# Four starting addresses for the four quarters of the transposed tokens

## The chip, the cores and the metric

The kernel runs on one core of one Trainium2 chip. The metric is the device time of one execution in microseconds. Three runs of the kernel before took 2196.5, 2198.72 and 2198.88 us; their median, 2198.72 us, is the time before. The profile shown below is of a separate execution of the same kernel, with a time of its own.

## The reference, cut to what matters

A decoder trunk of two layers on 256 tokens of width 2048, all in float32: a recurrent mixer with an MLP, then an attention mixer with an MLP, each with a norm ahead of it and a residual add behind it, and a final norm.

```python
for i in range(DEPTH):                     # DEPTH = 2
    h = _rmsnorm(x, mix_norm[i])
    x = x + (_rglru_block(h, ...) if i % 2 == 0 else _dilated_attention_block(h, ...))
    x = x + _mlp(_rmsnorm(x, mlp_norm[i]), mlp_w1[i], mlp_w2[i])
return _rmsnorm(x, final_norm)

def _mlp(h, w1, w2):                       # w1: 2048 x 8192, w2: 8192 x 2048
    u = jnp.square(jax.nn.relu(jnp.einsum('bsd,df->bsf', h, w1)))
    return jnp.einsum('bsf,fd->bsd', u, w2)
```

The recurrent block projects 2048 to 5120 (`w_in`), has block-diagonal gates, a scan over the tokens, and an output matrix of 2560 x 2048 (`w_out`). The attention block has `w_qkv` (2048 x 6144) and `w_o` (2048 x 2048). Every weight is used once, for all 256 tokens.

## The kernel before

Every weight matrix is cut on the host into units of 128 x 2048 floats (1 MB; the gates' units are half as large) and streamed through three buffers `raw`. ScalarE copies a unit to `whi` in the format that TensorE multiplies (L86), and VectorE subtracts, `wlo = raw - whi` (L90). Activations are split in the same way into a high and a low half. A product is then three matmuls: high by high, high by low, low by high. All of them go through one helper, `mm` (L142), so the profile has them on one line and tells them apart by the tiles that they read.

Two tiles carry activations into these products.

- `xT`, the tokens transposed: 2048 input rows as 16 blocks k of 128, in four tiles (quarters) `xT0` to `xT3` with four k each. A quarter has 4 x 512 floats per partition: for each k, 256 columns of high halves (one per token) and 256 of low halves. `new_xT` (L161) allocates a quarter; `transpose_chunk` (L169) fills it from the residual stream, once ahead of each of the three later sub-layers that need it, and the start of the program fills it from the host's transposed tokens.
- `aT0` to `aT19`, one tile of 512 floats for each 128 rows of a hidden activation: 256 high, 256 low.

There are two ways to multiply. In the *standing* way (`stand_w` L216, `stand_w2` L252) 128 x 128 of the weights is loaded into TensorE, and `xT` streams as the moving operand, in 256 or 512 columns; this serves `w_in` (40 units) and `w1` (64 units for each MLP, in four chunks of 16). In the *moving* way (`stand_x` L265) 128 columns of activations are loaded, and 512 columns of the weights stream; this serves `w_out`, `w2` and `w_o` with `aT`, and `w_qkv` (48 units) with `xT`. A moving unit covers four k, thus one quarter of `xT`; a standing unit covers all 16.

`stand_w2` has a style for each chunk, which sets the order of its matmuls (`orders`, L225). "h" is the high weights, "l" the low ones. For each k, "thirds" does h with the high columns, h with the low columns, l with the high columns, three matmuls of 256 columns that all add to the same 256 columns of `acc`; "thirds_low_first" starts with the l. The other styles do h with all 512 columns at once and l with 256, so that their sums come out in two halves: "wide_first" h, l; "as_was" l, h; "pairs" two k together (l, l, h, h); "fours" four h and then four l; "apart" all 16 h and then all 16 l. Columns and products are the same in each. `u_done` (L488) ends a tile: after one of the "thirds" kinds it reads 256 columns (L491), after the others it first adds the two halves (L493).

`stand_w` has the order of "thirds". The gates of the recurrent block (`gate_run`, L384) use it too, with a tile `chl` in the place of `xT`.

The order of everything is written out by hand: a list of items, one or two per unit. Before an item `before_unit` (L103) issues the loads and splits of units to come, and work on finished sums runs at fixed distances behind (`after`). Transposes (L176) and the two small transposes of `rstd_rows` (L209) run on TensorE between the items of the next chunk. Loads go through SP's queue alone.

Tiles of the pool `perm` lie one behind another in the order of first use, each rounded up to 32 bytes; the pool of the weights follows, and then the tiles of the current sub-layer. From this order and the sizes, the first bytes in a partition are:

| tile | start, bytes | modulo 512 |
|---|---|---|
| `xT0`, `xT1`, `xT2`, `xT3` | 45312, 53504, 61696, 69888 | 256 each |
| `aT0` to `aT15` | 80192 and every 2048 from there | 320 |
| `whi` (4 buffers), `wlo` (3 buffers) | 138560 and every 8192 from there | 320 |
| `chl` | 206176 | 352 |
| `aT16` to `aT19` | 220512 and every 2048 from there | 352 |

A block of 128 weights in a row is 512 bytes, a half of an activation block 1024 bytes. So for a given pair of tiles the distance modulo 512 between the moving operand and the loaded one is the same for every k and every buffer: -64 for `xT` against the weights, +32 for `chl` against the weights, and, with the weights moving, 0 against `aT0` to `aT15`, -32 against `aT16` to `aT19`, +64 against `xT`.

Of the kernel before, what the change touches and what calls it, by code (L numbers as in the profile page):

```python
# [11 lines left out]
F32R = mybir.dt.float32r  # L12
# [31 lines left out]
SOFT = (5, 3, 3, 3, 3)  # L44
LOOK_LO = 2
LOOK_HI = 3


@with_exitstack
def trunk(ctx: ExitStack, tc: tile.TileContext, a: dict, out: bass.AP):  # L50
    nc = tc.nc
    P = 128

    perm = ctx.enter_context(tc.tile_pool(name="perm", bufs=1))
# [7 lines left out]
    def unit(ap, width=UW):  # L62
        units.append((ap, width))
        return len(units) - 1
# [27 lines left out]
    def cut_hi(i):  # L92
        new_hi(i)
        for n in range(len(raw[i])):
            hi_piece(i, n)
# [7 lines left out]
    def before_unit(i):  # L103
        while seen["load"] < min(len(units), i + 1 + LOOK_LOAD):
            load(seen["load"])
            seen["load"] += 1
        while seen["hi"] < min(len(units), i + 1 + LOOK_HI):
            cut_hi(seen["hi"])
# [7 lines left out]
    def item(u, fn):  # L116
        items.append((u, fn))
# [20 lines left out]
    def after(n, fn, *args):  # L138
        later.setdefault(now[0] + n, []).append((fn, args))
# [13 lines left out]
    xc = [perm.tile([P, NT, 512], F32, name=f"xc{n}") for n in range(NCH)]  # L153
    ssq = perm.tile([P, NT, NCH], F32, name="ssq", bufs=2)
    state = {}

    def hilo(hi_out, lo_out, src):
        nc.scalar.activation(hi_out, src, AF.Copy)
        nc.vector.tensor_sub(lo_out, src, hi_out.bitcast(F32))

    def new_xT(n):  # L161
        t = perm.tile([P, 4, 512], F32R, name=f"xT{n}")
        state["xT", n] = t
        return t

# [3 lines left out]
    def transpose_chunk(n, gname):  # L169
        xg = perm.tile([P, 4, S], F32, name="xg", bufs=2)  # L170
        for b in range(2):
            tr = psum.tile([P, 2, S], F32, name="tr", bufs=2)
            for k in range(2):
                c = (2 * b + k) * 128
                for t in range(NT):
                    nc.tensor.transpose(tr[:, k, t * 128:(t + 1) * 128], xc[n][:, t, c:c + 128], ident)  # L176
            for k in range(2):
                nc.scalar.activation(xg[:, 2 * b + k, :], tr[:, k, :], AF.Identity,
                                     scale=pcol(gname, 4 * n + 2 * b + k))
        t = new_xT(n)  # L180
        for h in range(2):
            s = slice(2 * h, 2 * h + 2)
            hilo(t[:, s, 0:256], t[:, s, 256:512], xg[:, s, :])
# [68 lines left out]
    def stand_w2(ps, u, ks, w_at, first, last, style):  # L252
        hi, lo = split[u]
        todo = orders(style, ks)
        if first and todo[0][0] == "l" and not one_sum(style):

            at = next(i for i, p in enumerate(todo) if p[0] == "h")
            todo = [todo[at]] + todo[:at] + todo[at + 1:]
        for n, (w, k, c0, c1) in enumerate(todo):
            j = k - ks[0] + w_at  # L260
            s = slice(j * 128, (j + 1) * 128)
            o = ps[:, 0:256] if one_sum(style) else ps[:, c0:c1]
            mm(o, (hi if w == "h" else lo)[:, s], xT(k)[:, c0:c1], first and n == 0, last and n == len(todo) - 1)
# [12 lines left out]
    def acc_tile():  # L276
        return psum.tile([P, 512], F32, name="acc", bufs=4)
# [3 lines left out]
    def out_item(key, u, get, ks, first, last, done):  # L281
        def run():
            if first:
                accs[key] = [acc_tile() for _ in range(NT)]
            stand_x(accs[key], u, get, ks, first, last)
            if last:
                after(0, done, accs.pop(key))
        item(u, run)

    def add_x(n, acc):  # L290
        for t in range(NT):
            nc.vector.tensor_add(xc[n][:, t, :], xc[n][:, t, :], acc[t])  # L292

    def close_chunk(n, gname, rows):
        def done(acc):
            if n == 0:
                new_ssq()
            add_x(n, acc)
            if n < NCH - 1:
                square_sum(n)  # L300
            after(1, transpose_chunk, n, gname)
            if n == NCH - 1:
                after(1, square_sum, n)
                after(1, rstd_cols)
                if rows:
                    after(4, rstd_rows)
        return done
# [196 lines left out]
    def plan_mlp(w1, w2, done, styles):  # L504
        for c in range(4):
            us = []

            def part(j, ks, first, last, us=us, c=c, style=styles[c]):
                def run():
                    if first:  # L510
                        accs["u", j] = acc_tile()
                    stand_w2(accs["u", j], us[j], ks, ks[0], first, last, style)
                    if last:
                        after(1 if c == 0 and j == 0 else 0, u_done, j, accs.pop(("u", j)), style)
                item(us[j], run)

            us.extend(unit(w1[c * 16 + j]) for j in range(16))
            at = 0
            if c == 0:
                for j in range(2):  # L520
                    part(j, range(0, 12), True, False)
                for j in range(2):
                    part(j, range(12, 16), False, True)
                at = 2
            for j in range(at, 16):
                part(j, range(16), True, True)
            for n in range(NCH):
                last_c = c == 3
                if last_c and n == NCH - 1 and done is final_done:
                    final_items([unit(w2[(c * 4 + n) * 4 + kq]) for kq in range(4)])  # L530
                    continue
                for kq in range(4):
                    u = unit(w2[(c * 4 + n) * 4 + kq])
                    out_item(("m", n), u, aT, range(4 * kq, 4 * kq + 4), kq == 0, kq == 3,
                             done(n) if last_c else (lambda acc, n=n: add_x(n, acc)))
# [135 lines left out]
    def final_items(us):  # L671
        acc = {}

        def part(kq, ts):
            def run():
                if kq == 0:
                    for t in ts:
                        acc[t] = acc_tile()
                stand_x(acc, us[kq], aT, range(4 * kq, 4 * kq + 4), kq == 0, kq == 3, ts)
                if kq == 3:  # L680
                    for t in ts:
                        after(0, final_rows, acc[t], t)
            item(us[kq], run)

        part(0, range(NT))
        for t in range(NT):
            for kq in (1, 2, 3):
                part(kq, (t,))

    def load_g():  # L690
# [9 lines left out]
    item(None, lru.close)  # L700
    item(None, lambda: lru.open("mlp"))
    plan_mlp(a["w1_0"], a["w2_0"], lambda n: close_chunk(n, "mix1", False),
             ("thirds", "wide_first", "pairs", "apart"))
    item(None, lru.close)
    item(None, lambda: lru.open("att"))
    plan_att()
    item(None, lru.close)
    item(None, load_g)
    plan_mlp(a["w1_1"], a["w2_1"], final_done, ("thirds_low_first", "fours", "thirds", "as_was"))


    nc.sync.dma_start(par, a["par"])
# [16 lines left out]
    for n in range(NCH):  # L729
        xg[n] = perm.tile([P, 4, S], F32, name="xg", bufs=2)  # L730
        rs = [wts.tile([P, UW], F32, name="raw", bufs=RAW_BUFS) for _ in range(3)] if n == 0 else rs
        for h in range(2 if n == 0 else 1):
            w = 2 if n == 0 else 4
            nc.sync.dma_start(xg[n][:, h * w:(h + 1) * w, :], a["xT"][:, 4 * n + h * w:4 * n + (h + 1) * w, :])
            for i in range(3):
# [6 lines left out]
                raw[i].append((s, rs[i][:, s]))  # L742
                nc.sync.dma_start(rs[i][:, s], units[i][0][:, s])
        t = new_xT(n)
        for h in range(2 if n == 0 else 1):
            w = 2 if n == 0 else 4
# [151 lines left out]
```

## Time and profile before

| | |
|---|---|
| median of the runs | 2198.72 us (2196.5 to 2198.88, 3 runs) |
| the profiled execution | 2199.65 us, of which the span of its instructions is 2197.9 us |
| TensorE busy | 2175.3 us, 99% of the span, 12490 matmuls |
| weight loads (beside the matmuls) | 1910.4 us, 12490 |
| VectorE, ScalarE busy | 1280.0 us (58%), 1061.3 us (48%) |
| moved by DMA | 413.40 MB, 188 GB/s |
| granted TensorE clock | 0.996 |

How to read it: a busy TensorE is one with a matmul under way, not one at its peak, since a matmul's recorded duration contains a fixed latency that overlaps the next one. What a matmul costs is seen from the starts: first and last start of a group, divided by the steps between them. The view of a tile gives, for each kind of instruction, count, shortest, median and longest duration in ns, and the first and last start in us; the names of buffers and quarters are left out, so `xT0` to `xT3` are all `xT`.

| stretch of the trace, us | what runs there |
|---|---|
| 6 to 269 | recurrent block: `w_in` (standing) and gates |
| 269 to 384 | `w_out` (moving, with `aT`), the last gate |
| 384 to 1094 | first MLP: four chunks, `w1` standing and `w2` moving by turns |
| 1094 to 1387 | QKV (moving, with `xT`) and attention |
| 1387 to 1483 | `w_o` (moving, with `aT`) |
| 1483 to 2189 | second MLP, four chunks |

### The profile page before, as it was taken

How to read it: one execution, taken by the hardware profiler on the slowest of the kernel's cores; microseconds unless marked ns; L12 is line 12 of the kernel's file. 1: busy time of each engine (PE TensorE's matmuls, PEld its weight loads, DVE VectorE, ACT ScalarE, POOL GpSimd, SP SyncE). 2: the span in 40 equal slices, each digit the busy share in tenths (PEclk: the TensorE clock that was granted, in tenths of full speed). 3: DMA queues.
4: the chain of work that ended last, by engine and by line, in shares of the span. 5: the costliest groups of instructions: out<-in, count | busy, mean ns of one | idle time of the engine just before them, and what ended most of it. 6: DMA issues, size and time to landing. Idle time of an engine off the chain costs nothing.

```text
span 2197.9 us, 29494 instructions
## 1 busy us (share of the span) xinstructions
PE 2175.3 (99%) x12490; PEld 1910.4 (87%) x12490; DVE 1280.0 (58%) x1344; ACT 1061.3 (48%) x1163; POOL 78.3 (4%) x42
## 2 busy tenths in 40 slices
PE   7999999999999999999999999999999999999998
PEld 7999988998888888888888888889988889988886
DVE  8898855554564565565555555555546645545654
ACT  5787754543443343344445544555434434433442
POOL 2221100000000000000000000000000000000001
PEclk9999999999999999999999999999999999999999
DMA  6565555455555555555554445455555555555553
GB/s 219 211 211 194 194 207 189 175 192 191 191 183 201 185 188 197 189 189 194 181 192 166 159 174 183 161 188 199 200 195 181 198 196 184 186 193 189 191 192 115
DMA packets 61700, 413.40 MB, mean 188 GB/s; under 512 B 6784, under 2 KB 7168, under 8 KB 13440
## 3 DMA queue, kind: packets, MB, share of 16 engines
q1 hardware_dynamic: 61568, 411.51, 53.3%
q8 instruction: 98, 1.61, 0.3%
q14 instruction: 34, 0.28, 0.0%
HBM read 409.39 MB, written 2.10 MB: 187 GB/s over the span
## 4 chain that ended last, share of the span: by engine, by line
PE 96%; DVE 2%; ACT 1%; POOL 0%; DMA 0%; issue 0%; SPq 0%; DVEq 0%; ACTq 0%
PE acc L142 93%; PE g L142 1%; DVE wlo L90 1%; PE tr L176 0%; PE tr L568 0%; PE g L576 0%; DMA xg<-in_xT 0%; DVE xT L750 0%; PE tr L599 0%; POOL a L357 0%; ACT whi L86 0%; POOL c L358 0%; PE g L609 0%; PE g L608 0%; PE g L607 0%
## 5 line engine op out<-in xcount | busy, mean ns | idle before, releaser
L90 DVE TENSOR_TENSOR wlo<-raw,whi 128x2048 fp32r<-128x2048 f32 (+3 forms) x400 | 883.4, 2212 | 345.6 <-PE acc L142 267.9
L86 ACT ACTIVATE whi<-raw 128x2048 fp32r<-128x2048 f32 (+3 forms) x400 | 736.8, 1844 | 525.2 <-PE acc L142 437.6
L142 PE MATMUL acc<-xT,whi 128*128 128x256 f32 (+1 forms) x4064 | 882.7, 317 | 7.0 <-ACT whi L86 6.3
L142 PE MATMUL acc<-whi,aT 128*128 128x512 f32 x2624 | 813.9, 390 | 0.0
L142 PEld LDWEIGHTS acc<-xT,whi 128*128 128x128 f32 x4064 | 653.8, 190 | 46.4 <-ACT whi L86 6.7
L142 PE MATMUL acc<-xT,wlo 128*128 128x256 f32 x2672 | 654.9, 280 | 7.1 <-DVE wlo L90 6.8
L142 PEld LDWEIGHTS acc<-whi,aT 128*128 128x128 f32 x2624 | 492.6, 188 | 102.2
L142 PE MATMUL acc<-wlo,aT 128*128 128x512 f32 x1312 | 510.7, 389 | 0.0
L142 PEld LDWEIGHTS acc<-xT,wlo 128*128 128x128 f32 x2672 | 481.8, 190 | 27.6 <-DVE wlo L90 8.3
L142 PEld LDWEIGHTS acc<-wlo,aT 128*128 128x128 f32 x1312 | 246.3, 188 | 50.5
L142 PE MATMUL acc<-whi,xT 128*128 128x512 f32 x768 | 245.9, 395 | 0.0
L496 ACT ACTIVATE mu<-mr 128x256 f32<-128x256 f32 x128 | 53.5, 418 | 370.2 <-DVE mr L494 242.7
L142 PEld LDWEIGHTS acc<-whi,xT 128*128 128x128 f32 x768 | 144.3, 188 | 30.7
L142 PE MATMUL acc<-wlo,xT 128*128 128x512 f32 x384 | 150.4, 392 | 0.0
L493 DVE TENSOR_REDUCE mr<-acc 128x256 f32<-128x512 f32 x80 | 55.3, 692 | 156.1 <-PE acc L142 156.1
L292 DVE TENSOR_TENSOR xc<-xc,acc 128x512 f32<-128x512 f32 x78 | 53.2, 687 | 97.7 <-PE acc L142 97.7
L491 DVE SCALAR_TENSOR_TENSOR mr<-acc,rstdB 128x256 f32<-128x256 f32 x48 | 20.2, 424 | 112.9 <-PE acc L142 112.9
L142 PEld LDWEIGHTS acc<-wlo,xT 128*128 128x128 f32 x384 | 72.2, 188 | 15.1
L643 POOL TENSOR_TENSOR xc<-xc,gB 128x1024 f32<-128x1024 f32 x3 | 10.6, 3534 | 1879.9 <-DMA raw<-in_w 1843.4
L498 ACT ACTIVATE aT<-mu 128x256 fp32r<-128x256 f32 x128 | 53.6, 419 | 4.1
L502 DVE TENSOR_TENSOR aT<-mu,aT 128x256 fp32r<-128x256 f32 x128 | 53.4, 418 | 0.0
L189 ACT ACTIVATE junk<-xc 128x512 bf16<-128x512 f32 x32 | 20.2, 633 | 57.1 <-DVE xc L292 38.6
(143 smaller groups left out, 792.2 us busy)
## 6 DMA issues: line engine op xcount, KB each, us to landing
raw<-in_w SPq DMA_DIRECT2D x256, 1024.0 KB, 4.8
raw<-in_w_qkv SPq DMA_DIRECT2D x48, 1024.0 KB, 4.8
raw<-in_w_in SPq DMA_DIRECT2D x35, 1024.0 KB, 4.8
raw<-in_w_out SPq DMA_DIRECT2D x20, 1024.0 KB, 4.8
raw<-in_w_o SPq DMA_DIRECT2D x16, 1024.0 KB, 4.8
raw<-in_w_g SPq DMA_DIRECT2D x10, 512.0 KB, 3.3
raw<-in_w_in SPq DMA_DIRECT2D x11, 256.0 KB, 5.0
xc<-in_x SPq DMA_DIRECT2D x4, 512.0 KB, 5.7
```

Of the source, the lines that this page charges most:

```text
L86: nc.scalar.activation(split[i][0][:, s], r, AF.Copy)
L90: nc.vector.tensor_sub(split[i][1][:, s], r, split[i][0][:, s].bitcast(F32))
L142: nc.tensor.matmul(o, l, r, start=start, stop=stop, skip_group_check=True)
L189: nc.scalar.activation(junk, xc[n][:, t, :], AF.Square, accum_out=sq[:, t, n:n + 1])
L292: nc.vector.tensor_add(xc[n][:, t, :], xc[n][:, t, :], acc[t])
L491: nc.vector.scalar_tensor_tensor(r, ps[:, 0:256], 0.0, state["rstdB"], op0=OP.max, op1=OP.mult)
L493: nc.vector.tensor_reduce(r, ps.rearrange("p (b c) -> p c b", b=2), axis=AX.X, op=OP.add)
L496: nc.scalar.activation(uu, r, AF.Square)
L498: nc.scalar.activation(t[:, 0:256], uu, AF.Copy)
L502: nc.vector.tensor_sub(t[:, 256:512], uu, t[:, 0:256].bitcast(F32))
L643: nc.gpsimd.tensor_mul(xc[n], xc[n], state["gB"][:, None, n * 512:(n + 1) * 512].to_broadcast([P, NT, 512]))
```

## The change

Each quarter's tile becomes one row of 2048 floats and a pad, and the quarter's data start some floats behind its beginning. `XT_AT` holds the starts in floats (32, 128, 96 and 128 bytes), `XT_PAD` the floats added to the tile (32, 128, 96 and 256 bytes). The pads come to 512 bytes, so that all tiles behind the quarters move by 512 bytes and keep their remainder.

| quarter | starts at, bytes | modulo 512 | minus the weights' 320 |
|---|---|---|---|
| `xT0` | 45312 + 32 = 45344 | 288 | -32 |
| `xT1` | 53536 + 128 = 53664 | 416 | +96 |
| `xT2` | 61856 + 96 = 61952 | 0 | -320, the same as +192 |
| `xT3` | 70144 + 128 = 70272 | 128 | -192, the same as +320 |

With it, the styles of the chunks change: the first MLP has "as_was", "thirds", "thirds_low_first" and "apart" in place of "thirds", "wide_first", "pairs" and "apart"; the second has "thirds" in all four chunks in place of "thirds_low_first", "fours", "thirds" and "as_was". What is computed stays.

```diff
+XT_AT = (8, 32, 24, 32)
+XT_PAD = (8, 32, 24, 64)
...
     state = {}
+    xT_home = [None] * 4
...
     def new_xT(n):
-        t = perm.tile([P, 4, 512], F32R, name=f"xT{n}")
+        xT_home[n] = perm.tile([P, 2048 + XT_PAD[n]], F32R, name=f"xT{n}")
+        t = xT_home[n][:, XT_AT[n]:XT_AT[n] + 2048].rearrange("p (k c) -> p k c", k=4)
         state["xT", n] = t
         return t
...
     plan_mlp(a["w1_0"], a["w2_0"], lambda n: close_chunk(n, "mix1", False),
-             ("thirds", "wide_first", "pairs", "apart"))
+             ("as_was", "thirds", "thirds_low_first", "apart"))
...
-    plan_mlp(a["w1_1"], a["w2_1"], final_done, ("thirds_low_first", "fours", "thirds", "as_was"))
+    plan_mlp(a["w1_1"], a["w2_1"], final_done, ("thirds", "thirds", "thirds", "thirds"))
```

## The prediction

> **What bounds the kernel now.** I read the page first: how full TensorE is, and the chain that ended last.
>
> ```profile
> span 2197.9 us, 29494 instructions
> PE 2175.3 (99%) x12490; PEld 1910.4 (87%) x12490; DVE 1280.0 (58%) x1344; ACT 1061.3 (48%) x1163; POOL 78.3 (4%) x42
> ...
> PE acc L142 93%; PE g L142 1%; DVE wlo L90 1%; PE tr L176 0%; PE tr L568 0%; PE g L576 0%; DMA xg<-in_xT 0%; DVE xT L750 0%; PE tr L599 0%; POOL a L357 0%; ACT whi L86 0%; POOL c L358 0%; PE g L609 0%; PE g L608 0%; PE g L607 0%
> ```
>
> TensorE never rests, and 93% of the chain is line 142, the one helper through which every split matmul goes. So the time is the number of columns streamed times what a column costs, and the only lever this change has is that cost. I then asked for the matmuls that touch xT in two stretches that run the same instructions: a chunk of the second MLP in the style "thirds_low_first" (from its third unit on), and the one in "thirds".
>
> ```profile
> L142 PE MATMUL acc<-xT,wlo x176: 276/276/276, 1511.7 to 1571.2; 128*128 128x256 f32 x176
> ```
>
> ```profile
> L142 PE MATMUL acc<-xT,wlo x256: 281/281/281, 1834.7 to 1924.8; 128*128 128x256 f32 x128
> ```
>
> The columns are count, shortest, median and longest duration in ns, first and last start in us. There is one wlo matmul per 128 input rows (one k), so the spacing of the wlo rows is the time of a "triple", 768 streamed columns: (1571.2 - 1511.7)/175 = 0.340 us in the first, (1924.8 - 1834.7)/255 = 0.3533 us in the second. Equal shapes, tiles and distances; 276 against 281 ns in duration. I call them **floor** and **slow**: 0.0133 us apart per triple, 0.213 us per unit of 16. What switches between them shows where other matmuls cut in, here rstd_rows (L209) during the first units of that "thirds_low_first" chunk:
>
> ```profile
> 1494.24 0.40 PE L142 MATMUL acc<-xT,whi 128*128 128x256 f32 x2
> ...
> 1494.59 0.40 PE L142 MATMUL acc<-xT,whi 128*128 128x256 f32 x2
> ...
> 1495.18 0.38 PE L209 MATMUL tr<-con,rs 128*128 128x128 f32 x2
> ...
> 1496.21 0.39 PE L142 MATMUL acc<-xT,whi 128*128 128x256 f32 x2
> ...
> 1496.55 0.28 PE L142 MATMUL acc<-xT,whi 128*128 128x256 f32 x1
> ```
>
> The step is 0.35 us ahead of the cut and 0.34 behind it, and the row from 1511.7 shows that it stays so to the chunk's end. So at the present distance the stream has two stable modes, and an interruption can flip it.
>
> **What the present distances cost.** By the order of allocation xT starts at remainder 256 modulo 512 and the weights at 320: xT lies 64 bytes below. A chunk of 256 triples at the floor is 256 x 0.340 = 87.0 us. "wide_first" and "as_was" have 255 steps between the first and the last of their wide matmuls:
>
> ```profile
> L142 PE MATMUL acc<-xT,whi x256: 392/397/398, 562.6 to 652.7; 128*128 128x512 f32 x128
> ```
>
> ```profile
> L142 PE MATMUL acc<-xT,whi x256: 388/397/398, 2011.9 to 2101.9; 128*128 128x512 f32 x128
> ```
>
> That is 90.1/255 = 0.3533, +3.4 for the chunk, and 90.0/255 = 0.3529, +3.3. "pairs", "apart" and "fours":
>
> ```profile
> L142 PE MATMUL acc<-xT,whi x256: 388/394/398, 740.1 to 828.8; 128*128 128x512 f32 x128
> ```
>
> ```profile
> L142 PE MATMUL acc<-xT,whi x256: 388/394/398, 916.1 to 1002.8; 128*128 128x512 f32 x128
> L142 PE MATMUL acc<-xT,wlo x256: 276/276/283, 919.9 to 1004.8; 128*128 128x256 f32 x128
> ```
>
> ```profile
> L142 PE MATMUL acc<-xT,whi x256: 388/394/398, 1658.6 to 1746.7; 128*128 128x512 f32 x128
> L142 PE MATMUL acc<-xT,wlo x256: 276/276/282, 1659.6 to 1747.3; 128*128 128x256 f32 x128
> ```
>
> From first to last start and one matmul more: 88.9, 88.8 and 88.8 us, so +1.9, +1.8 and +1.8. "thirds" in the second MLP is slow throughout, +3.4; "thirds_low_first" for its first 32 triples, +0.4; and "thirds" in the first MLP for 224 triples, +3.0:
>
> ```profile
> L142 PE MATMUL acc<-xT,wlo x225: 281/281/281, 396.1 to 475.4; 128*128 128x256 f32 x113
> ```
>
> Together 19.0 us. The recurrent projections run at 276, the floor, and have nothing to win:
>
> ```profile
> L142 PE MATMUL acc<-xT,whi x97: 276/276/276, 208.9 to 225.2; 128*128 128x256 f32 x97
> ```
>
> Where the activations are held as weights and the weight matrix streams, there are three distances: QKV with xT (64 bytes), aT0 to aT15 (0) and aT16 to aT19 (32 bytes below):
>
> ```profile
> L142 PE MATMUL acc<-wlo,xT x24: 394/394/394, 1203.2 to 1219.0; 128*128 128x512 f32 x24
> ```
>
> ```profile
> L142 PE MATMUL acc<-wlo,aT x120: 389/389/389, 481.2 to 562.1; 128*128 128x512 f32 x120
> ```
>
> ```profile
> L142 PE MATMUL acc<-wlo,aT x8: 392/396/396, 378.8 to 383.7; 128*128 128x512 f32 x8
> ```
>
> At distance 0 three wide matmuls take (562.1 - 481.2)/119 = 0.680 us, exactly two floors. At 32 bytes 4.9/7 = 0.700. In QKV 15.8/23 = 0.687, 0.007 too much; 48 units of 8 such groups make 384 x 0.007 = 2.7 us. What the change can touch is 19.0 + 2.7 = **21.7 us**.
>
> **The change part by part.** Weights, aT and all other tiles keep their remainders, since the four pads come to 512 bytes. The quarters go from -64, all four, to -32, +96, +192 and +320. No wait, transfer or dependence moves.
>
> *What a distance costs.* The gates (chl as the moving operand) lie at +32, and the first xT matmuls after a gate show what a change of distance costs:
>
> ```profile
> 250.02 0.40 PE L142 MATMUL g<-chl,whi 128*128 128x256 f32 x2
> ...
> 252.82 0.40 PE L142 MATMUL acc<-xT,whi 128*128 128x256 f32 x2
> ...
> 253.18 0.39 PE L142 MATMUL acc<-xT,whi 128*128 128x256 f32 x2
> ...
> 253.52 0.39 PE L142 MATMUL acc<-xT,whi 128*128 128x256 f32 x2
> ```
>
> A gate's 8 triples take 252.82 - 250.02 = 2.80 us: 0.350, +0.010 per triple. aT16 to aT19 pay 0.020 per 1536 columns, the same per column. So 32 bytes cost 0.010 on either side, whichever operand is held. Quarters 0 and 1 (-32 and +96, odd multiples of 32) take that. Quarters 2 and 3 (multiples of 64) have no row near them; the multiples of 64 that there are cost 0 (distance 0), 0.0036 (QKV, half of 0.007) and 0 or 0.0133 (-64). Bounds 0 and 0.0133; I take 0.0018, between the first two, because both of these ran without the slow mode throughout. A unit then costs 4 x (0.010 + 0.010 + 0.0018 + 0.0018) = 0.094 us above the floor. 128 MLP units with 37 recurrent ones (the first three wait for in_xT and the splits, as the chain names them) make 165 x 0.094 = 15.6 us; bounds 0 and 165 x 0.213 = 35.1.
>
> *Change of distance inside a unit.* 253.18 - 252.82 = 0.36, then 0.34: 0.02 us. There are four changes per unit. Bounds 0 and 165 x 0.08 = 13.2; I take one paid change per unit, 3.3 us, nearer the lower bound, since "thirds" at 1834.7 was entered from aT with its step at 0.353 like all that follow.
>
> *QKV.* Each unit there holds one quarter: 24 units at 0.020 x 8 make 3.8 us, 24 at half of 0.007 x 8 make 0.7. Together 4.5 (bounds 0 and 48 x 0.16 = 7.7).
>
> *Styles.* The lists now hold three "thirds" kinds more; these cut each wide matmul in two, 768 matmuls and weight loads more. By the rows two and two floors are one: 0.340 for 768 columns cut, 0.680 for 1536 uncut, so the cut is free. It also drops 48 reductions on VectorE:
>
> ```profile
> L493 DVE TENSOR_REDUCE mr<-acc 128x256 f32<-128x512 f32 x80 | 55.3, 692 | 156.1 <-PE acc L142 156.1
> ```
>
> They wait for TensorE, not it for them: 48 x 0.692 = 33 us of VectorE's time with no gain; were the cover gone, it would be 0.7 us at the end of a chunk, for three chunks.
>
> *Sum.* 15.6 + 3.3 + 4.5 = 23.4 against 21.7: +1.7 us on the profiled execution's 2199.65 (its span and 1.75 around it). That one lies 0.9 above the median of 2198.72, so 2200.4 on the median's scale; **2200**.
>
> **Rivals.** *Far is free:* only -32 collides, +96 and beyond do not, and changes of distance cost nothing. For it: distance 0 and one mode of -64 are free, so the cost is not everywhere. Against it: +64 pays too, farther out than the 32-byte rows. 165 x 4 x 0.010 = 6.6, QKV 12 x 0.16 = 1.9: 8.5 against 21.7, so 2185.5.
>
> *All four free*, QKV too: 2198.7 - 21.7 = 2177. Only the floor at distance 0 speaks for it.
>
> *The slow mode everywhere:* each quarter pays 0.0133, and the recurrent units, at the floor today, lose it. Place: each matmul with xT; price 35.1 and 7.7 in QKV, 42.8 against 21.7: 2220. This side decides as soon as the mean over the quarters passes (21.7 - 4.5)/(165 x 16) = 0.0065 us per triple. For it: four changes of distance per unit are four interruptions, and an interruption switches modes. Against: the one shown switched to the floor.
>
> *The change does not do what it says:* distance is nothing, and the mode is a matter of what precedes. Then "as_was" 3.3, "apart" 1.8 and six chunks of the "thirds" kind at 3.4, one of which rstd_rows may cut to 0.4: 22.5 to 25.5 against 19.0, +3.5 to +6.5: 2204. For it: two modes at one distance. Against: the gate at 0.350 between recurrent stretches at 0.340. The Trainium skill (TensorE: Matmul & The Clock Gate, "Step-by-step: what each phase is for") says that TensorE reads the moving operand and the next weights through two independent ports, so that loading weights takes no bandwidth from the running matmul; by it this rival would hold. The trace's 276 and 281 ns for equal matmuls do not agree with it as it stands.
>
> **How the numbers follow.** Chances: the forecast 0.36, far free 0.24, all free 0.07, slow everywhere 0.13, distance nothing 0.17, none of these 0.03. The forecast's own range is 2194 to 2213 (changes of distance from 0 to 13.2, quarters 2 and 3 from 0 up to the QKV row). The range 2184 to 2216 takes in "far free" and "distance nothing" and leaves out "all free" and "slow everywhere", 0.2 in all. A measurement here tells about 0.2% (4.4 us) from nothing. Faster: 0.24 + 0.07 and 0.05 of the forecast, 0.36. Slower: 0.13, 0.09 of "distance nothing" and 0.12 of the forecast, 0.34. The same: 0.30.
>
> **What would show it.** In the four "thirds" chunks of the second MLP the spacing by k must repeat with the quarter: eight triples near 0.350, eight near 0.342. A flat 0.340 says all free, a flat 0.353 the slow mode; chunks of one style at different levels say that what precedes decides. QKV units must differ by kq: 0.700, 0.700, 0.683, 0.683. The recurrent units must leave the floor; if they stay at 276, I am too high by 3.5 us. The prediction fails above all if quarters 2 and 3 are slow (up to +15) or quarter 1 is free (-8).

## The result, and the profile after

The changed kernel takes **2218.61 us** (median of 3 runs, 2218.57 to 2219.89) against 2198.72 us: a ratio of 1.0096, with a 95% interval of 1.0073 to 1.0118. It is 19.9 us slower, where 1.3 us were forecast, and lies 2.6 us above the upper end of the range. The profiled execution's span grew from 2197.9 to 2216.8 us, at a granted clock of 0.998 (0.996 before).

The page of the changed kernel, span, engines and chain of waits:

```profile
span 2216.8 us, 31006 instructions
PE 2194.3 (99%) x13258; PEld 1960.0 (88%) x13258; DVE 1245.1 (56%) x1296; ACT 1061.3 (48%) x1163; POOL 77.5 (3%) x42
...
PE acc L145 93%; PE g L145 1%; PE tr L181 0%; DVE wlo L93 0%; PE tr L573 0%; PE g L581 0%; DMA raw<-in_w_in 0%; PE tr L604 0%; POOL a L362 0%; ACT whi L89 0%; DVE xT L755 0%; DMA xg<-in_xT 0%; POOL c L363 0%; PE g L614 0%; PE g L613 0%
```

The picture is that of before (line 145 is the old 142): the same 93% of the chain, and TensorE 19.0 us busier. There are 768 matmuls more, which is the number of wide ones that the new styles cut in two. The time in which TensorE rests is the same, 22.6 us before and 22.5 after (span minus busy). So nothing waits longer; what a column costs has gone up. The view of the tile xT shows it, for the third chunk of the second MLP ("thirds" before and after) and for four recurrent units:

```profile
L145 PE MATMUL acc<-xT,wlo x256: 276/279/285, 1852.3 to 1942.9; 128*128 128x256 f32 x128
...
L145 PE MATMUL acc<-xT,wlo x64: 276/279/286, 206.8 to 229.2; 128*128 128x256 f32 x64
```

(1942.9 - 1852.3)/255 = 0.3553 us per triple, and (229.2 - 206.8)/63 = 0.3556 in the recurrent block, where the kernel before ran at the floor of 0.340. The timeline of one unit of that chunk, at the first triple of each quarter and of the next unit:

```profile
1897.49 0.40 PE L145 MATMUL acc<-xT,whi 128*128 128x256 f32 x2
...
1898.91 0.40 PE L145 MATMUL acc<-xT,whi 128*128 128x256 f32 x2
...
1900.35 0.40 PE L145 MATMUL acc<-xT,whi 128*128 128x256 f32 x2
...
1901.76 0.40 PE L145 MATMUL acc<-xT,whi 128*128 128x256 f32 x2
...
1903.18 0.40 PE L145 MATMUL acc<-xT,whi 128*128 128x256 f32 x2
```

The steps are 1.42, 1.44, 1.41 and 1.42 us for four triples each, 0.355, 0.360, 0.3525 and 0.355 per triple: every quarter is well above the floor. In QKV, where a unit holds one quarter, four units in a row (quarters 2, 3, 0, 1) show:

```profile
L145 PE MATMUL acc<-wlo,xT x8: 392/392/392, 1212.9 to 1217.7; 128*128 128x512 f32 x8
...
L145 PE MATMUL acc<-wlo,xT x8: 394/394/394, 1218.4 to 1223.3; 128*128 128x512 f32 x8
...
L145 PE MATMUL acc<-wlo,xT x8: 393/395/397, 1224.0 to 1228.9; 128*128 128x512 f32 x8
...
L145 PE MATMUL acc<-wlo,xT x8: 392/396/400, 1229.6 to 1234.6; 128*128 128x512 f32 x8
```

Over seven steps that is 0.686, 0.700, 0.700 and 0.71, the last good to 0.01, as the view gives tenths of a microsecond: quarter 2 pays what all paid before, the other three pay about 0.020 per group, quarter 3 among them.

By stage, from the start of a stage's first matmul in the one trace and the other: the recurrent block with `w_out` took 384.1 us and takes 389.6 (+5.5), the first MLP 710.6 and 713.4 (+2.8), QKV and attention with `w_o` 388.3 and 392.0 (+3.7), the second MLP to the end 714.9 and 721.8 (+6.9). Together +18.9, the whole of the span.

In what follows, a stage's **excess** is the sum, over all matmuls with xT, of the time from one start to the next beyond 113.33 ns per 256 columns (the floor; a triple is 0.340); longer gaps, above 126 ns, count as waits and are left out. A wide matmul is counted with twice these numbers. By it the recurrent block went from 0.7 to 8.9 us, the eight MLP chunks from 19.0 to 28.4, QKV from 2.7 to 6.4. The waits of the recurrent block's start were 18.8 us before and 16.9 after. They lie between 12 and 19 us over all traces, in no order that follows the edits, so the time of a single execution can differ by some us for a reason that has nothing to do with an edit.

### The profile page after: what moved, and what is told of

The parts are those of the page before. It is cut to its first block, busy times and chain, and to the rows that moved or that the text cites. A ratio compares the mean times of both kernels' runs of the same rounds, so it can differ in the third digit from the quotient of the medians.

```text
span 2216.8 us, 31006 instructions
## 1 busy us (share of the span) xinstructions
PE 2194.3 (99%) x13258; PEld 1960.0 (88%) x13258; DVE 1245.1 (56%) x1296; ACT 1061.3 (48%) x1163; POOL 77.5 (3%) x42
## 4 chain that ended last, share of the span: by engine, by line
PE 96%; DVE 1%; ACT 1%; DMA 0%; POOL 0%; issue 0%; SPq 0%; DVEq 0%; ACTq 0%
PE acc L145 93%; PE g L145 1%; PE tr L181 0%; DVE wlo L93 0%; PE tr L573 0%; PE g L581 0%; DMA raw<-in_w_in 0%; PE tr L604 0%; POOL a L362 0%; ACT whi L89 0%; DVE xT L755 0%; DMA xg<-in_xT 0%; POOL c L363 0%; PE g L614 0%; PE g L613 0%
## 5 line engine op out<-in xcount | busy, mean ns | idle before, releaser
L145 PE MATMUL acc<-xT,whi 128*128 128x256 f32 (+1 forms) x4832 | 925.4, 294 | 7.5 <-ACT whi L89 5.4
L145 PEld LDWEIGHTS acc<-xT,whi 128*128 128x128 f32 x4832 | 760.1, 189 | 29.0 <-ACT whi L89 5.6
L145 PE MATMUL acc<-xT,wlo 128*128 128x256 f32 x2672 | 710.0, 281 | 6.4 <-DVE wlo L93 6.4
L145 PEld LDWEIGHTS acc<-xT,wlo 128*128 128x128 f32 x2672 | 489.6, 189 | 10.4 <-DVE wlo L93 7.5
L496 DVE SCALAR_TENSOR_TENSOR mr<-acc,rstdB 128x256 f32<-128x256 f32 x96 | 40.6, 424 | 254.8 <-PE acc L145 254.8
L498 DVE TENSOR_REDUCE mr<-acc 128x256 f32<-128x512 f32 x32 | 22.1, 690 | 56.6 <-PE acc L145 56.5
```

Of the source, the lines that this page charges most:

```text
L145: nc.tensor.matmul(o, l, r, start=start, stop=stop, skip_group_check=True)
L496: nc.vector.scalar_tensor_tensor(r, ps[:, 0:256], 0.0, state["rstdB"], op0=OP.max, op1=OP.mult)
L498: nc.vector.tensor_reduce(r, ps.rearrange("p (b c) -> p c b", b=2), axis=AX.X, op=OP.add)
```

## Experiments

Each is a change of the kernel after, unless it says otherwise. With one distance for all quarters the tiles lie as in the kernel before, moved together; the pads always come to 512 bytes. The kernel before took 2195.7 to 2196.4 us on the chips of these runs, so their differences are taken against that. Where neither a ratio nor a range is given, a kernel ran once. Ten executions of one kernel lie up to 6 us apart here, so a single time tells little by itself, and the reading rests on the spacings in the trace. The expectations count costs in cycles, 16 of which are 6.7 ns.

### All four quarters at distance 0

```diff
-XT_AT = (8, 32, 24, 32)
-XT_PAD = (8, 32, 24, 64)
+XT_AT = (16, 0, 0, 0)
+XT_PAD = (16, 0, 0, 112)
```

> The changed kernel with all four quarters at distance 0 from the weights, instead of -32, +96, +192 and +320. Theory one, the distance itself decides and 0 is free, as it is for aT0 to aT15: every standing unit at 0.340 us per triple whatever its style, QKV at 0.680 us per three wide matmuls, and with 21.7 us of such cost in the kernel before about 2177 us. Theory two, what precedes a stretch decides which mode it runs in, and the floor with aT belongs to the unbroken stream of wide matmuls: some chunks at 0.353, about 2200 us.

Measured: 2218.9 us against 2196.12, ratio 1.0106 (1.0091 to 1.0121). Neither expectation came true: the distance that cost nothing in the trace before, 0, is among the dearest of all that were run for a "thirds" chunk. The tile xT in a "thirds" chunk and in the "apart" chunk:

```profile
L145 PE MATMUL acc<-xT,whi x512: 278/283/283, 1850.0 to 1941.9; 128*128 128x256 f32 x171
...
L145 PE MATMUL acc<-xT,whi x256: 389/389/398, 925.3 to 1012.2; 128*128 128x512 f32 x128
L145 PE MATMUL acc<-xT,wlo x256: 277/283/283, 928.9 to 1014.2; 128*128 128x256 f32 x128
```

In the first row the 256 column matmuls last 283 ns, and the 512 rows span 255 triples and one matmul: 91.9 us, 0.360 per triple. In the "apart" chunk the 512 column matmuls are at 389, their floor, and the 256 column ones again at 283. QKV, all 512 columns wide, fell to an excess of 0.8 us. So the price of a distance depends on the width of the moving operand: distance 0 is nearly free for 512 columns and costs 6.7 ns for each matmul of 256. The reading of the aT rows as a price of the distance alone falls.

### The styles alone

```diff
-XT_AT = (8, 32, 24, 32)
-XT_PAD = (8, 32, 24, 64)
+XT_AT = (0, 0, 0, 0)
+XT_PAD = (0, 0, 0, 128)
```

> The changed kernel's styles with the quarters where they were, all at -64. If the distances made the loss: 2199 to 2205 us, the "thirds" chunks at 0.340 or 0.353 and the recurrent projections at 0.340. If the styles made it: about 2218 us.

Measured: 2200.06 us against 2196.12, ratio 1.0021 (1.0011 to 1.003). All quarters are at -64 again, and only the order of the matmuls differs from the kernel before. The chunks have an excess of 3.2 ("as_was"), 3.4, 3.4, 1.7 ("apart"), 0.4, 3.4, 3.4, 3.4: 22.3 us in place of 19.0. The second MLP's first and third chunk:

```profile
L145 PE MATMUL acc<-xT,wlo x256: 276/276/282, 1481.3 to 1569.5; 128*128 128x256 f32 x128
...
L145 PE MATMUL acc<-xT,wlo x256: 281/281/281, 1834.4 to 1924.5; 128*128 128x256 f32 x128
```

Both are "thirds"; the first is the one in which rstd_rows cuts in, and it left the slow mode there. So of the 19 to 20 us some 3.9 are the styles, and some 16 the distances. The pads move every other tile by the same 512 bytes as in the changed kernel, so that move is not what costs. In the recurrent block, which this edit does not touch, 13 of 39 units ran in the slow mode in this trace (3.0 us of excess) and one did in the trace before (0.7): the slow mode at -64 is not limited to the MLPs.

### Steps of 128 bytes

```diff
-XT_AT = (8, 32, 24, 32)
-XT_PAD = (8, 32, 24, 64)
+XT_AT = (16, 32, 32, 32)
+XT_PAD = (16, 32, 32, 48)
```

The quarters lie at 0, +128, +256 and +384.

> The changed kernel with quarters at 0, +128, +256 and +384. If each distance has its own cost, the quarter at 0 stays at the floor and the other three show what 128, 256 and 384 cost, each with a spacing of its own that repeats every unit. If it is the change of distance inside a unit that costs, all four quarters pay, the one at 0 too, and the recurrent units take about 5.69 us as in the changed kernel (5.44 at the floor).

Measured: 2220.07 us. QKV units of quarters 2, 3, 0, 1:

```profile
L145 PE MATMUL acc<-wlo,xT x8: 389/389/389, 1214.3 to 1219.0; 128*128 128x512 f32 x8
...
L145 PE MATMUL acc<-wlo,xT x8: 390/394/404, 1219.7 to 1224.6; 128*128 128x512 f32 x8
...
L145 PE MATMUL acc<-wlo,xT x8: 389/389/395, 1225.3 to 1230.1; 128*128 128x512 f32 x8
...
L145 PE MATMUL acc<-wlo,xT x8: 390/394/404, 1230.8 to 1235.7; 128*128 128x512 f32 x8
```

0 and +256 behave alike (389, the floor of a wide matmul), +128 and +384 alike (394). So in QKV distances count modulo 256 bytes, not 512. The standing units say little here: the four quarters cost 5.5, 5.6, 5.5 and 5.6 ns per 256 columns.

### All quarters at +192

```diff
-XT_AT = (8, 32, 24, 32)
-XT_PAD = (8, 32, 24, 64)
+XT_AT = (64, 0, 0, 0)
+XT_PAD = (64, 0, 0, 64)
```

> The changed kernel with all four quarters at +192. If each distance has its own cost: quarter 2 at +192 paid about 10 of the 11 to 12 cycles of the others in the changed kernel, so units near 5.65 us and about 2212 to 2216 us. If the changes of distance inside a unit cost, or throw the stream into the slow mode: the recurrent units return to 5.44 us and the time to 2180 to 2200 us.

Measured: 2198.31 us against 2196.12, and every chunk as at -64: 3.18, 3.40, 3.40, 1.69, 0.42, 3.40, 3.40, 3.40 us, QKV 2.71. The third chunk of the second MLP:

```profile
L145 PE MATMUL acc<-xT,wlo x256: 281/281/281, 1833.0 to 1923.1; 128*128 128x256 f32 x128
```

+192 is -64 modulo 256, and here the standing units show it too. Quarter 2 of the changed kernel was given its old distance. The second expectation's time came true, but not for its reason: it is this distance that has a floor, not the absence of changes of distance, as the next runs show.

### One distance each: -32, +96, +64, +128

```diff
-XT_AT = (8, 32, 24, 32)
-XT_PAD = (8, 32, 24, 64)
+XT_AT = (72, 0, 0, 0)
+XT_PAD = (72, 0, 0, 56)
```

`XT_AT` is given here for +224, modulo 256 the same as -32; the first number is 40 for +96, 32 for +64 and 48 for +128, and the pads always come to 128 floats.

> All four quarters at +224, which is -32 if distances count modulo 256 (as -64 and +192 being equal says); quarter 0 of the changed kernel. If each distance has a cost of its own: about 11.7 cycles per 256 columns as that quarter paid, units of 5.67 us against 5.44 at the floor, the recurrent projections too, about 2216 us. If the mix of distances pinned the stream in a slow mode: the recurrent projections at the floor again and 2180 to 2203 us.

> All four at +96, quarter 1 of the changed kernel, the dearest there. Own cost: 15.7 cycles per 256 columns, units of 5.75 us, about 2226 us. Mix: 2180 to 2203 us.

> All four at +64 (quarter 3 of the changed kernel, at +320, if distances count modulo 256). Own cost: 11.3 cycles per 256 columns, units of 5.67 us, about 2215 us. Mix: 2180 to 2203 us.

> All four at +128, which paid 13.5 cycles per 256 columns in the mix of 0 and 128, where 0 paid 13.1 though it pays 16.0 alone. Own cost: well below 16 or well above it, so that the mix is near the mean of the two: about 10.5 cycles, units of 5.65 us, 2212 us. Mix: nothing follows for 128 alone; floor or slow mode.

Measured, with the excess in us of a whole stage:

| all quarters at | us | recurrent | "thirds" chunk | "apart" chunk | QKV |
|---|---|---|---|---|---|
| -32 (quarter 0 of the change) | 2220.24 | 9.3 | 3.8 | 2.8 | 7.3 |
| +96 (quarter 1) | 2231.93 | 12.2 | 5.1 | 3.4 | 8.3 |
| +192, the same as -64 (quarter 2) | 2198.31 | 0.3 | 3.4 or 0.4 | 1.7 | 2.7 |
| +64 (quarter 3) | 2208.11 | 2.2 | 3.4 | 1.2 | 7.4 |
| mean of these four | | 6.0 | 3.9 | 2.3 | 6.4 |
| the changed kernel | 2218.61 | 8.9 | 3.9 | 2.5 | 6.4 |
| 0 | 2218.9 | 12.4 | 5.1 | 2.0 | 0.8 |
| +128 | 2224.38 | 9.9 | 5.1 | 2.9 | 6.8 |

The third chunk of the second MLP at -32:

```profile
L145 PE MATMUL acc<-xT,wlo x256: 277/280/285, 1854.0 to 1944.5; 128*128 128x256 f32 x128
```

At +96:

```profile
L145 PE MATMUL acc<-xT,wlo x256: 278/282/297, 1863.0 to 1954.8; 128*128 128x256 f32 x128
```

At +64:

```profile
L145 PE MATMUL acc<-xT,wlo x256: 279/279/282, 1842.8 to 1932.9; 128*128 128x256 f32 x128
```

By 255 steps: 0.3549, 0.3600 and 0.3533 us per triple, and 0.3533 at +192. Their mean is 0.3554; the changed kernel has 0.3553. Each distance alone costs what its quarter costs in the mixture, within what the timeline can tell (0.355, 0.360, 0.3525, 0.355). No cost of going from one distance to another is left over in these chunks or in QKV. Only the recurrent block pays more mixed than the mean of the four, 8.9 against 6.0. At +64 and +192 alone most of its units run at the floor, and in the mixture none does. Taking these two at the price of their slow mode (3.4/16 us per unit, 8.1 for 38 units) the mean is 9.4; that is an estimate, not a run.

The column "recurrent" is not fixed at -64: the five traces with all quarters there have 0.7, 1.6 to 1.7 (three) and 3.0 us, by how many of the early units are slow. And the interruption by rstd_rows, which frees the stream at -64 and +192 (0.4), leaves it slow at +64 (3.4).

That a mixture costs the mean of its parts is not general: steps of 128 mix two distances that cost 5.1 us per chunk alone, and cost 4.3 mixed. The expectation for +128, about 10.5 cycles (4.4 ns), was worked out from such a mean and missed: 6.7 ns were measured. Why was not found.

In all of these runs xT moves and the weights stay, so they do not by themselves tell the distance from xT's own address. One comparison in the traces speaks for the distance, with its sign. The wide matmuls of the "apart" chunk start every 232.9 ns at -64 and every 229.3 at +64. In QKV, where xT is held and the weights move, it is the other way round: 229.0 with xT at -64, 233.3 with xT at +64. Counted from the held operand to the moving one, it is 229 at +64 and 233 at -64 in both. For 256 columns no run makes this comparison.

### Interrupting the stream

Back at -64, "thirds" in all eight chunks, and one to seven transposes of the identity, 128 columns each into a buffer that nobody reads, ahead of every second unit from the fifth on:

```diff
-XT_AT = (8, 32, 24, 32)
-XT_PAD = (8, 32, 24, 64)
+XT_AT = (0, 0, 0, 0)
+XT_PAD = (0, 0, 0, 128)
...
+    def cut_of(c, j, w1):
+        q = c + (4 if w1 is a["w1_1"] else 0)
+        return (j // 2 + q) % 7 + 1 if j in (4, 6, 8, 10, 12, 14) else 0
...
+                    cut = cut_of(c, j, w1) if first else 0
+                    if cut:
+                        tr = psum.tile([P, 2, S], F32, name="tr", bufs=2)
+                        for _ in range(cut):
+                            nc.tensor.transpose(tr[:, 0, 0:128], ident, ident)
                     stand_w2(accs["u", j], us[j], ks, ks[0], first, last, style)
...
-             ("as_was", "thirds", "thirds_low_first", "apart"))
+             ("thirds", "thirds", "thirds", "thirds"))
```

> All quarters at -64 as in the kernel before, "thirds" in all eight MLP chunks, and ahead of units 4, 6, 8, 10, 12 and 14 of each chunk one to seven transposes of the identity on TensorE, another number each time (they compute nothing that is used). If a stretch keeps its mode until something cuts in, and a cut can throw it either way: behind some of the 48 cuts the step is 0.340 us per triple up to the next cut, behind others 0.353, constant in between; the time lies between 2180 and 2215 us. If the floor can only be entered from a gate: 0.353 behind all of them, about 2215 us (48 cuts of 0.1 to 0.9 us on top of 2203).

Measured: 2211.89 us, the transposes included. The timeline around a cut of one and around a cut of seven:

```profile
463.16 0.40 PE L145 MATMUL acc<-xT,whi 128*128 128x256 f32 x2
...
463.52 0.27 PE L525 MATMUL tr<-con 128*128 128x128 f32 x1
463.55 0.48 PE L145 MATMUL acc<-xT,whi 128*128 128x256 f32 x2
...
463.98 0.40 PE L145 MATMUL acc<-xT,whi 128*128 128x256 f32 x2
...
464.34 0.39 PE L145 MATMUL acc<-xT,whi 128*128 128x256 f32 x2
...
464.68 0.39 PE L145 MATMUL acc<-xT,whi 128*128 128x256 f32 x2
...
465.02 0.39 PE L145 MATMUL acc<-xT,whi 128*128 128x256 f32 x2
```

```profile
450.76 0.39 PE L145 MATMUL acc<-xT,whi 128*128 128x256 f32 x2
...
451.10 0.39 PE L145 MATMUL acc<-xT,whi 128*128 128x256 f32 x2
...
451.44 0.93 PE L525 MATMUL tr<-con 128*128 128x128 f32 x7
452.13 0.48 PE L145 MATMUL acc<-xT,whi 128*128 128x256 f32 x2
...
452.92 0.40 PE L145 MATMUL acc<-xT,whi 128*128 128x256 f32 x2
...
453.27 0.40 PE L145 MATMUL acc<-xT,whi 128*128 128x256 f32 x2
```

Behind the first the step is 0.34 us from the third triple on, and behind the second it goes from 0.34 to 0.35. Over the 48 cuts: of 15 made in the slow mode all 15 ended at the floor, whatever their length; of 33 made at the floor 10 ended slow (2 of 2 with one transpose, 2 of 3 with two, 1 of 4 with three, none of 17 with four to six, 5 of 7 with seven). Between two cuts the spacing never moved from 340.0 or 353.3 ns. So a mode keeps itself until something cuts in, and a cut sets it anew. That it is a phase between the stream of the moving operand and that of the weight loads is a reading that fits; no run shows the two streams themselves. One transpose costs about 0.11 us: 27 ns to the next matmul's start, and some 85 ns once behind that.

### "apart" in all chunks

```diff
-XT_AT = (8, 32, 24, 32)
-XT_PAD = (8, 32, 24, 64)
+XT_AT = (0, 0, 0, 0)
+XT_PAD = (0, 0, 0, 128)
...
-             ("as_was", "thirds", "thirds_low_first", "apart"))
+             ("apart", "apart", "apart", "apart"))
...
-    plan_mlp(a["w1_1"], a["w2_1"], final_done, ("thirds", "thirds", "thirds", "thirds"))
+    plan_mlp(a["w1_1"], a["w2_1"], final_done, ("apart", "apart", "apart", "apart"))
```

> All quarters at -64, the style "apart" in all eight MLP chunks. If a chunk costs what its style and distance cost, independent of its place: 8 times 1.7 us above the floor instead of 19.0, so 5.4 us faster than the kernel before. If place and entry decide: chunks that differ by up to 3.4 us, and a time within 3 us of the kernel before.

Measured: 2193.81 us (2190.41 to 2196.42) against 2195.72, ratio 0.9989 (0.998 to 0.9999). The chunks are at 1.69 to 1.76 each, 13.7 in place of 19.0, as the first expectation has it; the recurrent block, which the edit does not touch, has 1.6 in place of 0.7. The time fell by about 2 us, not by 5.4, and its interval reaches to 4.4, just what the sums give. By the time alone the second expectation (within 3 us) would do as well; the equal chunks are what speaks against it.

### One transpose where the stream is slow

At -64, "thirds" in all chunks, and a single transpose in each of the seven chunks that start slow:

```diff
-XT_AT = (8, 32, 24, 32)
-XT_PAD = (8, 32, 24, 64)
+XT_AT = (0, 0, 0, 0)
+XT_PAD = (0, 0, 0, 128)
...
+    def cut_at(c, w1):
+        if c == 0:
+            return 4 if w1 is a["w1_0"] else -1
+        return 1
...
+                    if first and j == cut_at(c, w1):
+                        tr = psum.tile([P, 2, S], F32, name="tr", bufs=2)
+                        nc.tensor.transpose(tr[:, 0, 0:128], ident, ident)
                     stand_w2(accs["u", j], us[j], ks, ks[0], first, last, style)
...
-             ("as_was", "thirds", "thirds_low_first", "apart"))
+             ("thirds", "thirds", "thirds", "thirds"))
```

> All quarters of xT at -64, as in the kernel before, and style "thirds" in all eight MLP chunks, whose two modes at this distance are 0.340 and 0.3533 us per triple. A single identity transpose stands ahead of the second unit of each chunk but the first of each MLP; in the first chunk of the first MLP it stands ahead of the fifth unit, and in the first chunk of the second MLP there is none, because the transposes of rstd_rows already leave it at the floor. Theory (two modes, and one transpose takes the stream out of the slow one; it did so in 5 of 5 cases): behind the transpose 0.340 us per triple to the end of each chunk, 0.3 to 0.6 us above the floor per chunk and about 1.5 in the first, some 5 us in place of 19.0; time about 2182. Rival (the slow mode comes back by itself, or the transpose switches it off only ahead of certain units): chunks at 3.4, time 2195 to 2200.

Measured: **2181.07 us** (2179.32 to 2182.87, 5 runs) against 2196.2, ratio 0.9933 (0.9919 to 0.9946): faster than both kernels. All seven transposes freed the stream. The page, and the tile xT in the third chunk of the second MLP:

```profile
span 2177.5 us, 32029 instructions
```

```profile
L145 PE MATMUL acc<-xT,wlo x256: 276/276/282, 1819.9 to 1906.9; 128*128 128x256 f32 x128
```

(1906.9 - 1819.9)/255 = 0.3412 with the transpose and the slow first unit in it; the kernel before has 0.3533 there. The chunks come to 2.4 us (0.7, six at 0.22, 0.4) in place of 19.0, which with seven times 0.11 for the transposes and 0.9 more in the recurrent block makes -14.9; measured is -15.1. The waits of the start, which differ from trace to trace, are left out of this sum.

### The same transposes in the changed kernel

```diff
+    def cut_at(c, w1):
+        return 4 if c == 0 else 1
...
+                    if first and j == cut_at(c, w1):
+                        tr = psum.tile([P, 2, S], F32, name="tr", bufs=2)
+                        nc.tensor.transpose(tr[:, 0, 0:128], ident, ident)
                     stand_w2(accs["u", j], us[j], ks, ks[0], first, last, style)
```

> The changed kernel with its four distances and its styles; a single identity transpose ahead of the second unit of each MLP chunk, ahead of the fifth in the first chunk of each MLP. Theory (each distance has its own price and, but for 64 and 192, no floor to return to): the mean spacing behind each transpose is what it was, near 118.5 ns per matmul, 0.3555 us per triple, and the time is 2217 to 2221. Rival (the mixture is only a slow mode, from which an interruption frees it): 0.340 to 0.345 per triple behind the transposes, and 2190 to 2205.

Measured: 2215.12 us in one run. The third chunk of the second MLP:

```profile
L145 PE MATMUL acc<-xT,wlo x256: 276/279/285, 1848.7 to 1939.4; 128*128 128x256 f32 x128
```

(1939.4 - 1848.7)/255 = 0.3557, against 0.3553 without the transpose. The chunks have an excess of 3.8 in place of 3.9, and in the "thirds" chunks the spacing settles behind the transpose at 118.47 ns per matmul, as without it. The time is 2 us below the expected 2217 to 2221 and 3.5 below the changed kernel's, which is not the stream: the waits at the recurrent block's start are 12.9 us in this trace and 16.9 in the other. So a transpose at this place frees nothing in the mixture, and the rival falls.

## Why the prediction was wrong

**What was right.** TensorE's rate is the only thing that moved: the chain kept its 93%, the 48 dropped reductions and the added matmuls brought no wait. The old costs, 19.0 and 2.7 us, are what the starts add up to, and the two modes and their flip are real: 15 of 15 cuts and the 15 us of the single transposes rest on them. The sign of the sum was right, its size not: +1.7 forecast, +18.9 in the span. The sign counts for little, since the prediction's own limit for telling a difference was 4.4 us.

**The step that failed** is the price of quarters 2 and 3. The prediction had no row near them, named 0 and 0.0133 us per triple as bounds and took 0.0018, from two rows (aT at distance 0, and QKV) in which the activations were held and 512 columns of weights moved. Measured in the mixture are 0.0124 and 0.0141, just under and just over the upper bound. In the prediction's sum the two quarters were 165 x 4 x 0.0036 = 2.4 us; at the measured prices they would be 165 x 4 x 0.0265 = 17.5. These 15 us are the largest miss in the sum, and the prediction had named this as what would break it ("up to +15"). Two reasons, each shown by a run: the rows taken do not carry over, because a distance has another price at 256 columns than at 512 (distance 0: 6.7 ns and nearly none); and quarter 2 at +192 has the distance of before, since only the remainder by 256 counts, so that it stayed where the slow mode is. Quarter 3 is at +64 by the same count, and alone that distance is slow in every "thirds" chunk too.

**Quarters 0 and 1** were taken at 0.010 each, from the gates at +32 and aT16 to aT19. They cost 0.0146 and 0.0196: -32 is dearer than +32 (the gates' 0.010 stayed), and "odd multiples of 32" is no class with one price. **The paid change of distance**, 3.3 us, has nothing left to pay for in the chunks and in QKV: the single distances already add up to the mixture. Standing units and changes together were 18.9 us; measured are 37.3, namely 28.4 in the MLPs and 8.9 in the recurrent block.

**The recurrent block** was named rightly as a place that could only lose, at 37 x 0.114 = 4.2 us; it lost 8.2 and gave 1.9 back in the waits of its start, which the prediction had as fixed. **QKV** was 4.5, measured 6.4: quarter 3 at +320, which is +64, pays 0.020 per group like the odd ones (all 48 units at +64 cost 7.4 us), and only quarter 2 keeps 0.007. **Styles** were costed at 0. Alone they cost 3.3 us in the chunks, 3.9 in the median time, because the kinds they replace were at 1.7 to 1.9 and "thirds" is at 3.4 whenever nothing cuts in. The rival "the change does not do what it says" had this sum (+3.5), and the forecast left it out because it let the new distances set the rate, whatever the style.

**The rivals.** "The slow mode everywhere" gave 2220 and a sum of 42.8; 2218.6 and 43.7 were measured, so its place and price were near. Its reason was not right, so the hit is partly luck: the mixture is not the slow mode of -64, since a transpose that frees the stream there does nothing here. Each distance has a price of its own, and of those run, only +64 and -64 (with +192) showed a floor for 256 columns. "Far is free" and "all four free" fall with the quarter steps. "Distance is nothing" falls with 2198 to 2232 us for one order of instructions. The rule of the Trainium skill behind it (TensorE: Matmul & The Clock Gate, "Step-by-step: what each phase is for") is that of two independent read ports, so that loading weights takes nothing from the running matmul. With 276 against 283 ns for equal matmuls at -64 and at 0 the traces do not agree with it as it stands. That the two operands collide is the plain reading of this, but no run moved the weights or took their loads away, so where they would collide stays open.

**The chances.** Slow by more than 0.2% had 0.34, and "slow everywhere" 0.13. That was too little: its point of decision, a mean of 0.0065 us per triple, lies below the 0.010 of every row with 256 columns that was not at -64, of which there was one, the gates.

## What to carry to other kernels

A price read from a trace holds for the width, the role (held or moving) and the address of the row it is from; before it is used for another, ask which of the three differs, and where two differ take the bound, not the middle. Where the starts of equal matmuls show two constant spacings, look at what stands at the point of change before moving any data: here "thirds" in all chunks with seven transposes that compute nothing was worth 15 us, and four new addresses cost about 16. A mixture of good and bad distances does not average to something safe; one distance at which a floor exists, with something that brings the stream to it, was the best of what was run. The transpose is no remedy in general: made where the stream is already at the floor, a single one threw it into the slow mode.

## What the runs showed of the hardware that was not expected

- The distance between the two operands counts modulo 256 bytes: 0 and +256 alike and +128 and +384 alike in QKV, and -64 and +192 equal to the hundredth of a microsecond in all eight chunks.
- For 512 columns the sign of the distance counts, from the held operand to the moving one: 229 ns from start to start at +64 and 233 at -64, whichever of the two xT is.
- What a matmul of 256 columns takes above its 113.33 ns: 6.7 ns at 0 and +96, 6.7 at +128 (5.4 in one chunk), 5.0 at -32, 4.4 or nothing at -64 and +64. For the wide ones of QKV, by xT's distance: some 0.7 ns at 0, 2.4 at -64, 6 to 7 at the others.
- At -64 two spacings, 340.0 and 353.3 ns per triple, each stable over hundreds of triples; a single 128 column transpose took the stream from the slow one to the floor in 5 of 5 and 7 of 7 cases, and from the floor to the slow one in 2 of 2.
- Not tried: +32 and +160 for xT, another address for the weights, and what in the fetch of the operands makes the two modes.
